# Weight sums of the down product made by copying and accumulating transfers from DRAM to DRAM

## The chip, the cores and the metric

The kernel runs on one core of a Trainium2 chip. The metric is the device time of one execution in microseconds. Before the change the median of three runs is 1769.81 us (1769.12 to 1770.55).

The engines have these names: PE is TensorE's matrix products, PEld its weight loads, DVE is VectorE, ACT is ScalarE, POOL is GpSimd and SP is SyncE. Transfers are issued by SP and by POOL, each in the order of its own queue, and all of them are carried by the same 16 DMA engines.

## What is computed

One step of a one-layer hybrid encoder over 1024 prompt frames and 32 sample frames with 1024 features. The parts that matter here, from the reference:

```
z = rms_norm(x, g_mix) @ w_in          # q, k, v, conv_h, conv_B, conv_C, gate_a, gate_b
a = attn_core(q, k, v) @ w_attn_out    # banded attention, 16 heads, sink softmax
...
x = x + (sigmoid(ga) * a + sigmoid(gb) * bo) @ w_mix_out
... (cross-attention into 256 memory tokens)
x = x + square(relu(rms_norm(x, g_mlp) @ w_up)) @ w_down
```

All inputs are float32, and the products are made from pairs of fp32r parts (a high part "h" and the rest "l"), three matrix products for one.

## The kernel before

The 1056 frames are columns, in three chunks of 384, 384 and 288. The kernel walks through stages, and in each the weights come one 128x1024 tile at a time: SP loads the raw tile, ACT makes its high part (L120), DVE its rest (L121), and TensorE multiplies. The order of the stages is the order of a list of items; within it a planner orders each engine's instructions by a timing model of its own. A call of `pin` puts an instruction behind everything that was traced before it on its engine; instructions traced later may still be planned ahead of it.

The stages that bear on this change, with their places in the trace of before:

- Start and first products, up to about 90 us.
- Attention, about 90 to 360 us. Sixteen host products (projections of q, k, conv and gates) of three chunks each give 48 slots. Into the slots are hung, as events, the parts of 36 attention units: scores (on TensorE, L560 and L561), the softmax (DVE L567, ACT L572, the reciprocal on DVE L576, the scaling of three of four heads on POOL L579 and of one on ACT L581), two slots later the transposes (TensorE L589), one more slot later the values (L601, L602). POOL also writes the sink columns (L563) and some conv and gate products (L631, L662).
- Paired input products, about 360 to 690 us, in which two products of 384 frames share their sub-products (L892 to L894); POOL adds weight tiles for them (L881 to L884).
- Attention output, about 690 to 760 us, then the conv, mix and cross-attention stages, then up and down.

The down product at the end also works with sub-products, in the manner of Strassen's scheme, and needs four combinations of the four blocks of each weight piece. With the blocks s0, s1, s2 and s3 of a piece they are s0+s2+s3, s0+s1+s2+s3, s0+s2 and s2+s3. There are 32 pieces of 128 x 4 x 256 numbers (512 KB), named by (j, t, i). The sums are made ahead, between the work of the first stages, and kept in DRAM in `wsum_d`; the down stage reads them from there by the keys "w_sum" (L138, from 1565 us on).

Before the change POOL makes each piece by one load into SBUF (L742), four additions (L749) and one store to `wsum_d` (L750). The loads go in turn into a tile "ws" of the stage's pool and into "xacc". `sum_step` stores the piece that was loaded last and loads the next one. It is called at 13 slots of the attention stage, by the steps of the paired products, and by the attention output's items, up to about 740 us.

POOL's queue holds its transfers' descriptors in a scratch area whose size is set where the program is made (line 1950, `dynamic_dma_scratch_size=1024`); the change leaves it as it is.

Of the kernel before, what the change touches and what calls it, by code (L numbers as in the profile page):

```python
# [10 lines left out]
F32 = mybir.dt.float32  # L11
F32R = mybir.dt.float32r
AF = mybir.ActivationFunctionType
ALU = mybir.AluOpType
# [4 lines left out]
P = 128  # L19
# [19 lines left out]
def hybrid_step(ctx: ExitStack, tc: tile.TileContext, io):  # L39
    nc = tc.nc  # L40
    act, dve, pool_e, pe, sp = nc.scalar, nc.vector, nc.gpsimd, nc.tensor, nc.sync
# [3 lines left out]
    def nm(s):  # L45
        uid[0] += 1
        return f"{s}_{uid[0]}"

    def opened(name, **kw):
        cm = tc.tile_pool(name=name, **kw)  # L50
        return cm, cm.__enter__()

    def closed(cm):
        cm.__exit__(None, None, None)
# [28 lines left out]
    wsum_d = dram.tile([4, 2, 4, P, 4, 256], F32, name="wsum_d")  # L83
# [4 lines left out]
    def pin(ins):  # L88
        return tc.keep_in_program_order(ins)

    def acc_tile(shape):
        return ps.tile(shape, F32, tag="acc", bufs=n_acc, name=nm("acc"))
# [16 lines left out]
    def item(fn, *keys):  # L109
        plan.append((fn, keys))  # L110
        worder.extend(keys)
# [85 lines left out]
    def xacc_tile():  # L197
        xacc[0] = tp.tile([P, 1056], F32, tag="xacc", name=nm("xacc"))
        return xacc[0]
# [215 lines left out]
    A = {}  # L415

    def open_att():
        closed(st_cm)
        A["cm"], A["pool"] = opened("att", bufs=1, reuse_waits="tile", side="right")
        C["pool"], C["bufs"] = A["pool"], 1  # L420
        W["pool"] = A["pool"]
        for i in range(2):
            for part in "hl":
                at_tile([P, 4 * P], F32R, f"PT{part}{i}")
        at_tile([P, 2, P], F32, "AO", 2)
        at_tile([64, 4, P], F32, "tO")
        at_tile([P, 4, 257], F32, "S", 2)
        at_tile([P, 1060], F32, "u")
        at_tile([P, 4, 256], F32, "ws")
        at_tile([P, 4, 256], F32, "bias")  # L430
        C["cvt"] = A["pool"].tile([P, 4, 4], F32, name="cvt")
        do_KS(0)
        do_KS_rest(0)

    def at_tile(shape, dt, tag, bufs=1):
        pool = kvp if tag in ("kt", "VS", "QA", "QB", "QC") else A["pool"]
        return pool.tile(shape, dt, tag=tag, bufs=bufs, name=nm(tag))
# [70 lines left out]
    def do_KS(kv):  # L508

        hi = at_tile([P, NT], F32R, "KSh", 2)  # L510
        lo = at_tile([P, NT], F32R, "KSl", 2)
        rows = slice(64 * (kv % 2), 64 * (kv % 2) + 64)
        src = ktt[kv // 2]
        for e in range(2):
            act.copy(hi[64 * e : 64 * e + 64], src[rows])
        for e in range(2):
            dve.tensor_sub(lo[64 * e : 64 * e + 64], src[rows], hi[rows].bitcast(F32))
        ksp[kv] = (hi, lo)

    def do_KS_rest(kv):  # L520
        ck = at_tile([P, P], F32, "ck")
        sp.dma_start(ck, io["cache_k"][:, kv])
        b = at_tile([P, 4, 256], F32, "bias")
        sp.dma_start(b, io["bias"][kv])
        bs = at_tile([P, 256], F32, "biass")
        sp.dma_start(bs, io["bias_s"][kv])
        ch = at_tile([P, P], F32R, "ckh")
        cl = at_tile([P, P], F32R, "ckl")
        split(ch, cl, ck)
        ksp[kv] += (ch, cl, b, bs)  # L530
# [156 lines left out]
    def in_emit(tile):  # L687
        which, f = tile
        return gate_emit(which, f) if which in "ab" else conv_emit(which, f)

    def in_col(tile):
        which, f = tile
        return 10 + 8 * "HBCab".index(which) + f

    def do_in(tile, extras=(), chunks=range(3)):
        def fn(w):
            emit = in_emit(tile)
            for c in chunks:
                n = CH[c][1]
                if tile[0] == "B":  # L700
                    conv_taps(tile[1], c)
                a = acc_tile([P, n])
                gemm(a, w, xg[c])
                emit(c, a)
                after(extras, c)

        return fn
# [20 lines left out]
    def at(slot, fn):  # L728
        events.setdefault(slot, []).append(fn)

    W = {}
    pieces = [(j, t, i) for j in range(4) for t in range(2) for i in range(4)]

    def sum_load(acc):
        W["acc"] = acc
        if pieces:
            at = pieces.pop(0)
            if acc:
                t = xacc_tile()[:, :1024].rearrange("p (q c) -> p q c", q=4)
            else:  # L740
                t = W["pool"].tile([P, 4, 256], F32, tag="ws", name=nm("ws"))
            pin(pool_e.dma_start(t, io["w_down"][at]))  # L742
            W["new"] = at, t

    def sum_add(old):
        if old:
            at, t = old
            for to, x, y in ((3, 2, 3), (2, 0, 2), (0, 0, 3), (1, 1, 0)):
                pin(pool_e.tensor_tensor(t[:, to], t[:, x], t[:, y], op=ALU.add))  # L749
            pin(pool_e.dma_start(wsum_d[at], t))  # L750

    def sum_step():
        old = W.pop("new", None)
        sum_load(not W.get("acc", True))
        sum_add(old)

    def sum_done():
        sum_add(W.pop("new", None))

    for kv, starts in enumerate([(0, 1, 2, 4, 5, 6, 8, 9, 10)] * 3 + [(0, 1, 2, 3, 4, 5, 6, 7, 8)]):  # L760
        base = (0, 12, 23, 34)[kv]
        units = [Unit(kv, p) for p in range(9)]
        for unit, k in zip(units, starts):
            at(base + k + 3, unit.values)
        for unit, k in zip(units, starts):
            at(base + k, unit.scores)
        for unit, k in zip(units, starts):
            at(base + k + 2, unit.turn)
        if kv < 3:
            at(base + 7, lambda kv=kv: do_KS(kv + 1))  # L770
            at(base + 11, lambda kv=kv: do_KS_rest(kv + 1))
        for k in ((5, 8, 11), (2, 5, 8, 11), (2, 5, 8, 11), (2, 5))[kv]:
            at(base + k, sum_step)
    at(44, sum_done)
    at(38, lambda: x_raw(0))
    at(40, lambda: x_sums(0))
    at(42, lambda: x_raw(1))
# [206 lines left out]
    def x_steps(i):  # L984
        if i == 0:
            todo = {"B11": lambda: x_issue(1, 4), "W4": lambda: x_issue(1, 3), "W2": lambda: [x_issue(1, 2), x_fetch(2), x_issue(2, 1)]}
        elif i == 1:
            todo = {"W4": lambda: x_issue(2, 4), "W3": lambda: x_issue(2, 3), "W2": lambda: x_issue(2, 2)}
        else:
            todo = {f"W{k}": lambda k=k: x_issue(i + 1, k) for k in (1, 4, 3, 2)}  # L990
            todo["B11"] = lambda: x_fetch(i + 1)

        def after(what):
            if what == "B11":
                sum_done()
            todo.get(what, lambda: None)()
            if what == "W3" and (i % 5):
                sum_load(True)
            if what == "B11" and XP[i][0][0] == "a" and "cv_cm" in S:
                closed(S.pop("r2_cm"))  # L1000
                closed(S.pop("cv_cm"))
                G["pool"] = ctx.enter_context(tc.tile_pool(name="gb", bufs=5, reuse_waits="tile", side="right"))

        return after
# [57 lines left out]
    def open_y(*_):  # L1062
        closed(S["pw_cm"])
        closed(S["tk_cm"])
        W["cm"], W["pool"] = opened("wsum", bufs=1, reuse_waits="tile")
        Y["pool"] = ctx.enter_context(tc.tile_pool(name="ypool", bufs=16, reuse_waits="tile", side="right"))

    todo = []
# [1 line left out]
    def loads(n):  # L1070
        for dst, src, c, k in [todo.pop(0) for _ in range(min(n, len(todo)))]:
            load_split(dst, src, c, k)

    def do_attn_out(f, chunks, steps):
        def fn(w):
            for c in chunks:
                n = CH[c][1]
                a = acc_tile([P, n])
                gemm(a, w, aop[c])
                t = tmp(n)  # L1080
                dve.tensor_mul(t, a, sg[c][f])  # L1081
                sp.dma_start(m1_d[c][:, f], t)
                for at, e in steps:
                    if at == c:
                        e()

        return fn
# [2 lines left out]
    item(lambda: todo.extend((aop, ao_d, c, k) for c in range(3) for k in range(NF)))  # L1090
    last = [t for pair in XP[len(XP) - LATE :] for t in pair]
    for t in last:
        item(do_in(t, [(2, lambda: loads(4)), (2, sum_step)], (2,)), ("w_in", in_col(t)))
    for f in range(4):
        chunks = range(3) if f else (0, 1)
        item(do_attn_out(f, chunks, [(0, sum_step if f == 0 else sum_done)]), ("w_attn_out", f))
    for f in range(4, NF):
        item(do_attn_out(f, (0,), []), ("w_attn_out", f))
    item(lambda: todo.extend((bcp, bc_d, 0, k) for k in range(NF)))
# [3 lines left out]
    for f in range(4, NF):  # L1103
        item(do_attn_out(f, (1,), [(1, lambda: loads(2))]), ("w_attn_out", f))
    run()
    assert not pieces and "new" not in W
    todo.extend((bcp, bc_d, 1, k) for k in range(NF))
    closed(W["cm"])
    closed(x_cm)
    xacc_tile()  # L1110

# [864 lines left out]
```

## Time and profile before

| what | value |
|---|---|
| median of three runs | 1769.81 us |
| the profiled execution | 1767.74 us |
| its span | 1766.0 us |
| PE busy | 1733.7 us, 98% |
| DVE busy | 1213.3 us, 69% |
| POOL busy | 657.9 us, 37% |
| POOL's transfers in all (q0) | 33.56 MB, 5.4% of the 16 DMA engines' span |
| SP's transfers in all (q1) | 276.97 MB, 47.2% |

Busy times are of one profiled execution, which is timed apart from the runs of the median. A group of instructions in the profile stands as line, engine, operation, what it writes and reads, the number of instructions, then their busy time and the mean in ns, then the engine's idle time ahead of them and what ended it. A row of transfers ends with the KB of one and the median time from issue to landing. A row of waits has the total in us, the number of times and the longest. A row of the timeline or the chain begins with the start and the length in us.

### The profile page before, as it was taken

How to read it: one execution, taken by the hardware profiler on the slowest of the kernel's cores; microseconds unless marked ns; L12 is line 12 of the kernel's file. 1: busy time of each engine (PE TensorE's matmuls, PEld its weight loads, DVE VectorE, ACT ScalarE, POOL GpSimd, SP SyncE). 2: the span in 40 equal slices, each digit the busy share in tenths (PEclk: the TensorE clock that was granted, in tenths of full speed). 3: DMA queues.
4: the chain of work that ended last, by engine and by line, in shares of the span. 5: the costliest groups of instructions: out<-in, count | busy, mean ns of one | idle time of the engine just before them, and what ended most of it. 6: DMA issues, size and time to landing. Idle time of an engine off the chain costs nothing.

```text
span 1766.0 us, 30039 instructions
## 1 busy us (share of the span) xinstructions
PE 1733.7 (98%) x11008; PEld 1711.6 (97%) x11008; DVE 1213.3 (69%) x2130; ACT 846.1 (48%) x1625; POOL 657.9 (37%) x702
## 2 busy tenths in 40 slices
PE   8999999999999999999999999999999999999997
PEld 8999999999999999999999999999999999999997
DVE  6768888777887767367576877666666675445665
ACT  8667767852232245144465755642222353432553
POOL 2246675643744534402324241375544300100111
PEclk9999999999999999999999999999999999999998
DMA  5413434442322527789766767744443497544674
GB/s 183 146 58 106 141 114 147 139 153 98 132 86 96 177 102 263 261 255 320 259 218 208 242 219 240 253 166 155 130 139 124 149 316 221 176 152 141 230 240 134
DMA packets 178115, 313.01 MB, mean 177 GB/s; under 512 B 18192, under 2 KB 137776, under 8 KB 177840
## 3 DMA queue, kind: packets, MB, share of 16 engines
q1 hardware_dynamic: 168320, 276.97, 47.2%
q0 software_dynamic: 9216, 33.56, 5.4%
q8 instruction: 86, 1.41, 0.3%
q10 hardware_dynamic: 432, 0.58, 0.1%
q14 instruction: 61, 0.50, 0.1%
HBM read 233.23 MB, written 77.81 MB: 176 GB/s over the span
## 4 chain that ended last, share of the span: by engine, by line
PE 72%; DMA 9%; DVE 6%; ACT 5%; issue 3%; POOL 2%; SPq 1%; POOLq 0%; DVEq 0%; ACTq 0%
PE acc L176 7%; PE acc L178 7%; PE acc L177 7%; PE acc L892 7%; PE acc L894 7%; PE acc L893 7%; PE acc L1707 5%; PE acc L1706 5%; PE acc L1708 5%; PE pa L177 3%; PE pa L178 3%; PE pa L176 3%; DVE wl L121 2%; ACT wh L120 1%; PE pt L589 1%
## 5 line engine op out<-in xcount | busy, mean ns | idle before, releaser
L120 ACT CAST wh<-wr 128x1024 fp32r<-128x1024 f32 (+1 forms) x224 | 234.1, 1045 | 311.4 <-PE acc L1707 77.1
L121 DVE TENSOR_TENSOR wl<-wr,wh 128x1024 fp32r<-128x1024 f32 (+1 forms) x224 | 307.3, 1372 | 93.2 <-ACT wh L120 91.7
L176 PE MATMUL acc<-Y,wh 128*128 128x384 f32 (+1 forms) x624 | 201.9, 324 | 2.6 <-DVE ct L1081 1.5
L178 PE MATMUL acc<-Y,wl 128*128 128x384 f32 (+1 forms) x624 | 201.6, 323 | 0.3 <-DVE wl L121 0.3
L177 PE MATMUL acc<-Y,wh 128*128 128x384 f32 (+1 forms) x624 | 201.6, 324 | 0.0
L253 POOL TENSOR_TENSOR xacc<-xacc,ct 128x384 f32<-128x384 f32 (+1 forms) x62 | 78.0, 1257 | 322.2 <-ACT ct L251 319.8
L176 PE MATMUL acc<-X,wh 128*128 128x384 f32 (+1 forms) x528 | 172.6, 327 | 1.2 <-ACT wh L120 1.2
L177 PE MATMUL acc<-X,wh 128*128 128x384 f32 (+1 forms) x528 | 171.8, 325 | 0.9 <-DVE X L257 0.9
L178 PE MATMUL acc<-X,wl 128*128 128x384 f32 (+1 forms) x528 | 171.0, 324 | 0.0
L176 PEld LDWEIGHTS acc<-Y,wh 128*128 128x128 f32 x624 | 117.0, 188 | 3.9 <-DVE ct L1081 1.9
L178 PEld LDWEIGHTS acc<-Y,wl 128*128 128x128 f32 x624 | 117.2, 188 | 0.6 <-DVE wl L121 0.6
L177 PEld LDWEIGHTS acc<-Y,wh 128*128 128x128 f32 x624 | 117.1, 188 | 0.0
L579 POOL TENSOR_SCALAR S<-S,rec 128x256 f32<-128x256 f32 (+1 forms) x96 | 93.3, 984 | 62.1 <-DVE rec L576 61.9
L1706 PE MATMUL acc<-Y,wh 128*128 128x384 f32 (+1 forms) x352 | 113.1, 321 | 0.2 <-ACT Y L120 0.2
L1707 PE MATMUL acc<-Y,wh 128*128 128x384 f32 (+1 forms) x352 | 113.1, 321 | 0.1
L1708 PE MATMUL acc<-Y,wl 128*128 128x384 f32 (+1 forms) x352 | 112.9, 321 | 0.0
L120 ACT CAST wh<-s 128x1024 fp32r<-128x1024 f32 x54 | 56.6, 1051 | 105.9 <-PE acc L893 72.3
L177 PEld LDWEIGHTS acc<-X,wh 128*128 128x128 f32 x528 | 100.0, 189 | 2.9 <-DVE X L257 1.8
L176 PEld LDWEIGHTS acc<-X,wh 128*128 128x128 f32 x528 | 99.8, 189 | 2.2 <-ACT wh L120 1.4
L178 PEld LDWEIGHTS acc<-X,wl 128*128 128x128 f32 x528 | 99.8, 189 | 1.0 <-DVE wl L121 0.2
L121 DVE TENSOR_TENSOR Y<-ct,Y 128x384 fp32r<-128x384 f32 (+1 forms) x128 | 68.9, 570 | 28.7 <-ACT Y L120 28.5
L120 ACT CAST Y<-ct 128x384 fp32r<-128x384 f32 (+1 forms) x128 | 59.2, 486 | 60.0 <-DMA ct<-bc_d 14.8
(405 smaller groups left out, 5360.3 us busy)
## 6 DMA issues: line engine op xcount, KB each, us to landing
wr<-in_w_in SPq DMA_DIRECT2D x55, 512.0 KB, 3.6
wr<-in_w_up SPq DMA_DIRECT2D x48, 512.0 KB, 3.8
wr<-in_w_down SPq DMA_DIRECT2D x32, 512.0 KB, 4.0
wr<-wsum_d SPq DMA_DIRECT2D x32, 512.0 KB, 3.5
wl<-wl_d SPq DMA_DIRECT2D x28, 512.0 KB, 4.8
wr<-in_w_conv_out SPq DMA_DIRECT2D x24, 512.0 KB, 4.5
wr<-in_w_mix SPq DMA_DIRECT2D x24, 512.0 KB, 4.7
xacc<-in_w_down POOLq DMA_DIRECT2D x21, 512.0 KB, 3.9
```

The source lines that it names most:

```text
L120: act.copy(hi, src)
L121: dve.tensor_sub(lo, src, hi.bitcast(F32))
L176: pe.matmul(out, wh[:, a], hi, start=(k == 0), stop=False)
L177: pe.matmul(out, wh[:, a], lo, start=False, stop=False)
L178: pe.matmul(out, wl[:, a], hi, start=False, stop=(k == len(acts) - 1))
L579: pool_e.tensor_scalar_mul(stl[:, h, :nk], stl[:, h, :nk], rec[:, h : h + 1])
L892: pe.matmul(acc, wh[:, a], hi, start=(start and k == 0), stop=False, skip_group_check=True)
L893: pe.matmul(acc, wh[:, a], lo, start=False, stop=False, skip_group_check=True)
L894: pe.matmul(acc, wl[:, a], hi, start=False, stop=(k == 3), skip_group_check=True)
L1706: pe.matmul(a, wh[:, s], hi, start=(start and k == 0), stop=False, skip_group_check=True)
L1707: pe.matmul(a, wh[:, s], lo, start=False, stop=False, skip_group_check=True)
L1708: pe.matmul(a, wl[:, s], hi, start=False, stop=(stop and k == len(acts) - 1), skip_group_check=True)
```

## The change

The tile "ws", the loads, the additions and the stores are gone. Two pieces are now taken together as 256 rows, which makes 16 pairs, and each pair goes through four phases, all of them transfers of POOL's queue from DRAM to DRAM. Phase 0 copies blocks 0 and 1 of the weights into targets 0 and 1, and blocks 0 and 3 into targets 2 and 3 (512 KB each). Phase 1 adds block 2 to targets 2 and 3, phase 2 adds target 3 to targets 0 and 1, phase 3 adds block 0 to target 1 (256 KB each). The additions are done by the transfers themselves (`accum_op`). The phases of the pairs are interleaved: the list holds phase 3 of one pair, phase 2 of the next, phase 1 of the one after it, phase 0 of a fourth, and so on. The 64 phases are issued in slots 4 to 43 of the attention stage, two in a slot where k % 5 is 0, 2 or 4 and one in the others. The calls in the paired products and in the attention output are taken out.

```diff
@@ open_att
-        W["pool"] = A["pool"]
...
-        at_tile([P, 4, 256], F32, "ws")
@@ the sums
-    def sum_load(acc):
...
-            pin(pool_e.dma_start(t, io["w_down"][at]))
-            W["new"] = at, t
-
-    def sum_add(old):
...
-            for to, x, y in ((3, 2, 3), (2, 0, 2), (0, 0, 3), (1, 1, 0)):
-                pin(pool_e.tensor_tensor(t[:, to], t[:, x], t[:, y], op=ALU.add))
-            pin(pool_e.dma_start(wsum_d[at], t))
...
+    def sum_phase(at, phase):
+        j, t, i = at
+        src, dst = io["w_down"][j, t, i : i + 2], wsum_d[j, t, i : i + 2]
+        src, dst = (x.rearrange("i p q c -> (i p) q c") for x in (src, dst))
+        wide = lambda x: x.to_broadcast([2 * P, 2, 256])
+        if phase == 0:
+            pin(pool_e.dma_start(dst[:, 0:2], src[:, 0:2]))
+            pin(pool_e.dma_start(dst[:, 2:4], src[:, 0:4:3]))
+        elif phase == 1:
+            for q in (2, 3):
+                pin(pool_e.dma_start(dst[:, q], src[:, 2], accum_op=ALU.add))
+        elif phase == 2:
+            for q in (0, 1):
+                pin(pool_e.dma_start(dst[:, q], dst[:, 3], accum_op=ALU.add))
+        else:
+            pin(pool_e.dma_start(dst[:, 1], src[:, 0], accum_op=ALU.add))
+
+    sums = [(j, t, i) for j in range(4) for t in range(2) for i in (0, 2)]
+    phases = [(sums[s - ph], ph) for s in range(len(sums) + 3) for ph in (3, 2, 1, 0) if 0 <= s - ph < len(sums)]
+
+    def sum_step(n=1):
+        for _ in range(min(n, len(phases))):
+            sum_phase(*phases.pop(0))
@@ the attention slots
-        for k in ((5, 8, 11), (2, 5, 8, 11), (2, 5, 8, 11), (2, 5))[kv]:
-            at(base + k, sum_step)
-    at(44, sum_done)
+    for k in range(4, 44):
+        at(k, lambda k=k: sum_step(1 + (k % 5 in (0, 2, 4))))
@@ paired products, attention output
-            if what == "B11":
-                sum_done()
...
-            if what == "W3" and (i % 5):
-                sum_load(True)
...
-        W["cm"], W["pool"] = opened("wsum", bufs=1, reuse_waits="tile")
...
-        item(do_in(t, [(2, lambda: loads(4)), (2, sum_step)], (2,)), ("w_in", in_col(t)))
+        item(do_in(t, [(2, lambda: loads(4))], (2,)), ("w_in", in_col(t)))
...
-        item(do_attn_out(f, chunks, [(0, sum_step if f == 0 else sum_done)]), ("w_attn_out", f))
+        item(do_attn_out(f, chunks, []), ("w_attn_out", f))
...
-    closed(W["cm"])
```

More of the change, by code (lines that the diff above doesn't have):

```diff
@@ L729, in at @@
         events.setdefault(slot, []).append(fn)
-    W = {}
-    pieces = [(j, t, i) for j in range(4) for t in range(2) for i in range(4)]
-    def sum_load(acc):
[L735 to L742, printed above, removed]
-            W["new"] = at, t
-    def sum_add(old):
-        if old:
-            at, t = old
-            for to, x, y in ((3, 2, 3), (2, 0, 2), (0, 0, 3), (1, 1, 0)):
[L749 to L758, printed above, removed]
+    def sum_phase(at, phase):
[19 more added lines that the diff above has]
+            sum_phase(*phases.pop(0))
     for kv, starts in enumerate([(0, 1, 2, 4, 5, 6, 8, 9, 10)] * 3 + [(0, 1, 2, 3, 4, 5, 6, 7, 8)]):
@@ L1105, in hybrid_step @@
     run()
-    assert not pieces and "new" not in W
+    assert not phases
     todo.extend((bcp, bc_d, 1, k) for k in range(NF))
-    closed(W["cm"])
     closed(x_cm)
```

## The prediction

> **What bounds the kernel now.** I read the page's shares of busy time first, then busy time by stretch over the whole span, to see which stretches still have idle TensorE time, because only that can be won.
>
> ```profile
> span 1766.0 us, 30039 instructions
> PE 1733.7 (98%) x11008; PEld 1711.6 (97%) x11008; DVE 1213.3 (69%) x2130; ACT 846.1 (48%) x1625; POOL 657.9 (37%) x702
> ...
> 120.00:350.00 230.00, 229.93 (x1522) 222.84 (x1521) 187.93 (x503) 171.03 (x437) 151.93 (x204) 1.00 0.38 128
> 350.00:440.00 90.00, 87.59 (x543) 86.14 (x543) 64.18 (x92) 40.62 (x68) 37.85 (x39) 1.00 0.38 126
> 440.00:700.00 260.00, 260.00 (x1634) 260.00 (x1634) 199.40 (x264) 89.61 (x126) 127.95 (x141) 1.00 0.40 138
> 700.00:760.00 60.00, 58.31 (x357) 57.67 (x356) 26.31 (x39) 15.79 (x24) 20.43 (x29) 1.00 0.77 256
> ...
> 930.00:1200.00 270.00, 260.22 (x1702) 254.36 (x1701) 197.13 (x347) 151.42 (x293) 107.42 (x95) 1.00 0.66 223
> ```
>
> In the rows by stretch the columns after the length are PE, PEld, DVE, ACT and POOL busy, the granted clock, the DMA share and GB/s. TensorE has no idle time in the attention stretch (120 to 350) or in 440 to 700, 2.4 us in 350 to 440 and 1.7 us in 700 to 760. So the four stretches in which the weight sums are made hold 4.1 us of idle TensorE time in all. The changed code can hardly win more than that; what it can lose has no such limit.
>
> Next I read the groups of POOL in the attention stretch, and the transfers in it.
>
> ```profile
> L579 POOL TENSOR_SCALAR S<-S,rec 128x256 f32<-128x256 f32 x75 | 76.8, 1036 | 39.4 <-DVE rec L576 39.2
> L749 POOL TENSOR_TENSOR ws<-ws 128x256 f32<-128x256 f32 x24 | 19.3, 806 | 0.9
> L749 POOL TENSOR_TENSOR xacc<-xacc 128x256 f32<-128x256 f32 x24 | 19.0, 792 | 1.1
> ...
> L742 POOL DMA_DIRECT2D ws<-in_w_down x7 | 4.2, 593 | 9.4 <-DMA wsum_d<-ws 9.4
> ...
> L750 POOL DMA_DIRECT2D wsum_d<-ws x6 | 3.7, 613 | 1.0 <-POOL ws L749 1.0
> L742 POOL DMA_DIRECT2D xacc<-in_w_down x6 | 3.6, 604 | 0.0
> L750 POOL DMA_DIRECT2D wsum_d<-xacc x6 | 3.6, 600 | 1.5 <-POOL xacc L749 1.5
> ```
>
> POOL's own duty here is the scaling of the softmax rows (L579), and its turn is tight. The next rows show POOL's third scaling, which ends at 340.76, and the transpose on TensorE that reads the result 0.4 us later.
>
> ```profile
> 338.03 2.73 POOL L579 TENSOR_SCALAR S<-S,rec 128x256 f32<-128x256 f32 x3 [0.80 <-DVE rec L576]
> ```
>
> ```profile
> 341.16 0.27 PE L589 MATMUL pt<-ident,S 128*128 128x128 f32 x1
> ```
>
> The chain of waits, read between 308 and 322, passes through POOL without a break, so here POOL is already the engine that the end hangs on.
>
> ```profile
> 309.52 1.81 POOL S L579 x2
> 311.33 0.57 POOL xacc L742
> ...
> 311.93 0.75 POOL ws L749
> ...
> 315.44 1.83 POOL S L579 x2
> ```
>
> **The change, part by part.** *Removed:* 128 additions (L749), 32 loads and 32 stores. Of these the attention stretch has 48 additions (38.3 us) and 25 transfers (15.1 us), 53.4 of POOL's 151.9 us. What stays is 98.5 us in 230, or 105 us in 245. The additions that stood behind 440 are worth nothing, since TensorE is full up to 700; those near 700 to 760 at most the 1.7 us.
>
> *Moved:* every sum now lies in slots 4 to 43 of the attention host items, and none behind them. The first load of before stands at slot 5 and the thirteenth at slot 39:
>
> ```profile
> 123.70 0.77 POOL L742 DMA_DIRECT2D ws<-in_w_down  x1
> ...
> 332.41 0.59 POOL L742 DMA_DIRECT2D ws<-in_w_down  x1
> ```
>
> 208.7 us for 34 slots is 6.1 us a slot, so 40 slots are 245 us. SP issues nothing new, and the reading of the sums starts long after, so no wait moves there. The tile "ws" and a use of "xacc" go; nothing waits for them at these places but POOL.
>
> *Added:* 16 pairs of pieces, each with 2 copies and 2 + 2 + 1 accumulating transfers: 112 transfers instead of the stretch's 25. The issue of one is 0.6 us (593 to 613 ns above, for 128 runs). The new ones have 256 runs, the second copy 512 on its reading side, and no row shows how the issue grows with runs; the ends are 0.6 and, in proportion to 256 runs, 1.2 us. I take 0.6: 67 us. POOL then has 105 + 67 = 172 of 245 us without any hold, which fits, with 73 us to spare.
>
> *Holds.* What decides is whether POOL is held at an issue until an earlier transfer of its own has landed, because the scalings (L579), the sink columns (L563) and the conv and gate products (L662, L631) are queued behind it, and TensorE's transposes wait for the first. Before, this happened 12 times in 64 transfers, 39.7 us, a mean of 3.3 us:
>
> ```profile
> POOL ws L742 <- DMA wsum_d<-ws: 21.5, 6, 6.0
> ...
> POOL xacc L742 <- DMA wsum_d<-xacc: 18.2, 6, 7.2
> ```
>
> There it cost nothing: the 13 loads of this stretch lie 17 us apart (208.7 us over 12), and the 9.4 us of such waits in it left TensorE full. Now there are 2.8 transfers to a slot. Behind another of the same slot stand the second transfer of phases 1 and 2 (32) and the first of a second phase in the 24 slots that run two (24): 56. The two copies of phase 0 I count as flying together. The price of one hold is the landing less the issue. No row shows a transfer from DRAM to DRAM or an accumulating one:
>
> ```profile
> wr<-in_w_in SPq DMA_DIRECT2D x13, 512.0 KB, 3.3
> ws<-in_w_down POOLq DMA_DIRECT2D x7, 512.0 KB, 3.9
> ao_d<-AO SPq DMA_DIRECT2D x27, 128.0 KB, 1.8
> ...
> wsum_d<-ws POOLq DMA_DIRECT2D x6, 512.0 KB, 3.1
> ```
>
> An accumulate of 256 KB reads 512 KB, its source and its target, and writes into DRAM. Its ends are 1.8 us (128 KB, half of what it writes) and 3.9 us (as much read, on this queue); I take 3.5, the mean of POOL's 512 KB load and 512 KB store. A hold is then 2.9 us, and 56 are 162 us. Some of them pass while POOL would have had nothing to do and some while pieces of other work lie between two transfers of one slot; that other work fills 43% of the stretch (105 of 245), and I let a third of the holds vanish in this way: 108 us.
>
> The rows show no hold that comes from anything but a tile's reuse. The Trainium skill ("DMA: Bandwidth & Descriptors", section "Terms") has 16-byte descriptors that GpSimd writes into rings in SBUF; the kernel's 1024 bytes of scratch (line 1950) would be 64 places by it, and by "Collectives: The Full Stack", section "The bandwidth ceiling: the fold count and why AG ≠ RS ≠ AR", an addition reads through two descriptors for each chunk. By both, my estimate for an accumulate is 33 places on each engine, so that two don't fit and the second waits for the first. No run here shows it yet. The first of these pages, section "Anatomy of one DMA — SWDGE (gpsimd) path", also prices a transfer at 2.0 us plus bytes over 436 GB/s, 2.6 us for 256 KB; by that the sum below would end at +2 us. Its price for 512 KB is 3.2 us, where the rows have 3.1 and 3.9.
>
> *Sum.* 105 + 67 + 108 = 280 us of POOL in 245 us: TensorE waits 35 us, spread over the stage. Profiled, 1767.7 + 35 = 1803 us. The profiled execution (span 1766.0 us and 1.7 around it) lies 2.1 us below the runs' median of 1769.8, so the forecast for the median is 1805 us. The far ends: landing 3.9 and nothing hidden is 56 x 3.3 = 185, with 172 it is 357, +112 us, 1882; landing 1.8 is 56 x 1.2 = 67, which fits, +0. If an issue cost 1.2 us, another 67 us would come on top; I leave that outside the range.
>
> **The rivals.**
>
> *No holds, or short ones (no change).* The dependent phases of a pair lie three phases apart, about 11 us, far beyond a landing of 3 to 4 us. If transfers of one phase fly together, or land in 2.6 us (two thirds of 56 x 2.0 = 75 us, about the 73 to spare), POOL keeps up and TensorE stays full: 1769.8. For it speaks that the holds of before left TensorE full, the longest of 6.0 us among them; against it the 0.4 us shown above. The same time comes out if the planner pulls the scalings ahead of the transfers, which are only kept behind what was traced before them: then the transfers run late, into the stage behind, where POOL has room. The change would then not do its work where it says.
>
> *Transfers too slow for the 16 engines (slower).*
>
> ```profile
> q1 hardware_dynamic: 14110, 16.10, 21.4%
> q0 software_dynamic: 3600, 13.11, 16.2%
> ```
>
> Before, 13.11 MB took 16.2% of 230 us, 2.84 us for a MB. 16.8 MB of copies and 21.0 MB of accumulates, counted twice for their two reads, are 58.7 MB, 167 us, 68% of 245 us; with the other queue's 21% that is just below full, and no loss. If an accumulate costs twice that again, it is 286 us and 52 of the other queue, 338 in 245: +93, about 1863. Nothing in the rows asks for the factor.
>
> *Faster.* The additions are gone, POOL is never late, and all 4.1 us of idle time in 350 to 440 and 700 to 760 goes: 1765.7. If the new plan also takes half of the 9.8 us in 930 to 1200, 1760.8. For it speaks that POOL's additions lie on the chain at 311 to 316; against it that TensorE was full there, and that the longest waits of TensorE in those two stretches are on DVE:
>
> ```profile
> PE acc L176 <- DVE ct L1081: 1.5, 1, 1.5
> ...
> PE acc L892 <- DVE ct L678: 1.0, 1, 1.0
> ```
>
> **How the numbers follow.** Holds that overfill POOL 0.47; transfer engines full 0.10; no holds, short holds or transfers put late 0.32; faster 0.11. A measurement of this kernel tells about 0.2%, 3.5 us, from no change. Slower by more than that: 0.57 from the first two, a little more for small losses in the third and a little less for a first case that ends near 0, so 0.57. Within: 0.32. Faster: 0.11. Range: the likeliest case alone is 1774 to 1882; down to the no-change case and part of the faster one it is 1764, and I keep 1882 above, leaving out some 5% below and 13% above.
>
> **What would show it.** Right: POOL's DMA rows longer than 0.6 us, or idle time before them that ends at a transfer to wsum_d; TensorE in 120 to 400 with tens of us idle before the transposes (L589), released by POOL; later stretches as before, only shifted. The additions (L749) gone from 440 to 760 with TensorE unchanged there shows that they cost nothing. Wrong: POOL issues of 0.6 us with no idle time before them and TensorE still full, or the accumulates lying behind 400. If TensorE waits for weights instead (L138 landing late, DMA share above 0.9), the second rival holds.

## The result and the profile after

The changed kernel takes 2029.78 us (median; 2026.03 to 2031.54) beside 1770.18 us for the kernel before in the same session: a ratio of 1.1476, with an interval of 1.1462 to 1.149. It is 259.6 us slower. The forecast was slower, by the right mechanism, but only by 35 us; the time lies far outside the stated range.

First the page's shares of busy time and the busy time by stretch, after the change:

```profile
span 2024.1 us, 29970 instructions
PE 1794.0 (89%) x11008; PEld 1754.8 (87%) x11008; DVE 1197.7 (59%) x2130; ACT 848.6 (42%) x1629; POOL 600.4 (30%) x622
...
115.00:640.00 525.00, 331.84 (x1780) 304.63 (x1778) 200.09 (x544) 192.08 (x477) 195.48 (x255) 0.78 0.54 108
640.00:700.00 60.00, 51.01 (x302) 50.70 (x303) 44.78 (x60) 23.19 (x35) 21.75 (x17) 0.90 0.32 111
700.00:1020.00 320.00, 320.00 (x2004) 320.00 (x2003) 219.55 (x312) 109.25 (x157) 63.22 (x63) 1.00 0.33 107
```

The columns of a row by stretch are those of the prediction's rows. From 700 us on TensorE is full through the paired products, as before (320.0 of 320 us). The loss lies in the attention stage, which now fills 115 to 640. The scalings of the softmax rows on POOL (one line of code, L579 before and L577 after, and its first and last start) date it:

```profile
L579 POOL TENSOR_SCALAR S<-S,rec x96: 593/924/1994, 95.3 to 349.2; 128x256 f32<-128x256 f32 x84, 128x128 f32<-128x128 f32 x12
```

```profile
L577 POOL TENSOR_SCALAR S<-S,rec x96: 592/948/2308, 94.3 to 608.3; 128x256 f32<-128x256 f32 x84, 128x128 f32<-128x128 f32 x12
```

The last scaling starts 259.1 us later, as much as the whole loss. What POOL did in between stands in its groups between 115 and 640; the part behind the bar is its idle time ahead of the group, and what ended it:

```profile
L577 POOL TENSOR_SCALAR S<-S,rec 128x256 f32<-128x256 f32 x76 | 76.9, 1174 | 13.3 <-DVE rec L574 13.2
L740 POOL DMA_DIRECT2D wsum_d<-in_w_down x32 | 29.8, 930 | 96.4 <-issue 90.9 <-DMA wsum_d<-in_w_down 5.5
L743 POOL DMA_DIRECT2D wsum_d<-wsum_d x32 | 29.3, 917 | 108.0 <-issue 108.0
L745 POOL DMA_DIRECT2D wsum_d<-in_w_down x16 | 15.3, 954 | 58.8 <-issue 46.1 <-DMA wsum_d<-wsum_d 9.9 <-PE acc L178 1.5
L737 POOL DMA_DIRECT2D wsum_d<-in_w_down x16 | 15.0, 935 | 49.0 <-issue 43.7 <-PE acc L178 4.5 <-PE pt L587 0.7
L736 POOL DMA_DIRECT2D wsum_d<-in_w_down x16 | 14.4, 899 | 0.0
```

POOL stands idle for 312 us ahead of its own transfers, 289 of them put down to "issue" (77 times), that is, to nothing that the profile names. With the 195 us of its busy time that is 484 of the 525 us; only 17 us of idle time stand ahead of the scalings and 23 us ahead of transfers for other reasons. The low share of 30% busy time hides this, because waiting at an issue isn't counted as busy. The stage's other engines wait for it: ACT's exponentials (L570) for the sink columns (L561), which stand in POOL's order behind the transfers, and TensorE's transposes for the scalings of POOL and of ACT. The two rows of TensorE are 142 of its 193 idle us in this stretch:

```profile
ACT S L570 <- POOL S L561: 185.8, 23, 15.0
PE pt L587 <- POOL S L577: 95.3, 24, 12.8
PE pt L587 <- ACT S L579: 46.4, 7, 12.7
```

The transfers that hold it, with KB each and the median time to landing, and POOL's timeline over the first of them:

```profile
wsum_d<-in_w_down POOLq DMA_DIRECT2D x32, 512.0 KB, 5.7
...
wsum_d<-in_w_down POOLq DMA_DIRECT2D x48, 256.0 KB, 5.1
```

```profile
123.17 1.03 POOL L740 DMA_DIRECT2D wsum_d<-in_w_down  x1 [5.47 <-DMA wsum_d<-in_w_down]
128.16 0.90 POOL L740 DMA_DIRECT2D wsum_d<-in_w_down  x1 [3.96 <-issue]
...
129.03 3.26 POOL L577 TENSOR_SCALAR S<-S,rec 128x256 f32<-128x256 f32 x3
132.02 0.85 POOL L736 DMA_DIRECT2D wsum_d<-in_w_down  x1
133.60 0.93 POOL L737 DMA_DIRECT2D wsum_d<-in_w_down  x1 [0.73 <-PE pt L587]
...
140.25 1.00 POOL L743 DMA_DIRECT2D wsum_d<-wsum_d  x1 [5.51 <-issue]
144.68 0.90 POOL L743 DMA_DIRECT2D wsum_d<-wsum_d  x1 [3.43 <-issue]
```

Here the second accumulating transfer of a phase starts 5.0 us after the first, which landed 4.7 us after its issue; further down it is 4.4 us. The scalings at 129.03 stand behind it in POOL's order. A plain copy (L736, 132.02) is issued 3.9 us after an accumulating transfer that takes 5.1 us to land, and isn't held.

### The profile page after: what moved, and what is told of

Read it like the earlier page. It is cut to its first block, busy times and chain, and to the rows that moved or that the text cites. A ratio compares the mean times of both kernels' runs of the same rounds, so it can differ in the third digit from the quotient of the medians.

```text
span 2024.1 us, 29970 instructions
## 1 busy us (share of the span) xinstructions
PE 1794.0 (89%) x11008; PEld 1754.8 (87%) x11008; DVE 1197.7 (59%) x2130; ACT 848.6 (42%) x1629; POOL 600.4 (30%) x622
## 3 DMA queue, kind: packets, MB, share of 16 engines
q0 software_dynamic: 26368, 37.76, 11.1%
## 4 chain that ended last, share of the span: by engine, by line
PE 63%; issue 16%; POOL 9%; DVE 4%; DMA 4%; ACT 3%; SPq 0%; POOLq 0%; ACTq 0%; DVEq 0%
PE acc L176 6%; PE acc L177 6%; PE acc L178 6%; PE acc L885 6%; PE acc L887 6%; PE acc L886 6%; PE acc L1694 5%; PE acc L1693 5%; PE acc L1695 5%; POOL S L577 4%; PE pa L177 2%; PE pa L176 2%; PE pa L178 2%; POOL wsum_d L740 1%; DVE wl L121 1%
## 5 line engine op out<-in xcount | busy, mean ns | idle before, releaser
L587 PE MATMUL pt<-ident,S 128*128 128x128 f32 x248 | 61.0, 349 | 158.1 <-POOL S L577 95.3
L587 PEld LDWEIGHTS pt<-ident,S 128*128 128x128 f32 x248 | 38.2, 173 | 175.0 <-POOL S L577 105.1
L176 PE MATMUL acc<-X,wh 128*128 128x384 f32 (+1 forms) x528 | 183.0, 347 | 0.8 <-ACT wh L120 0.8
L177 PE MATMUL acc<-X,wh 128*128 128x384 f32 (+1 forms) x528 | 181.3, 343 | 1.1 <-DVE X L257 1.1
L178 PE MATMUL acc<-X,wl 128*128 128x384 f32 (+1 forms) x528 | 181.0, 343 | 0.0
L570 ACT ACTIVATE S<-S,nmx 128x257 f32<-128x257 f32 (+1 forms) x132 | 63.9, 487 | 194.0 <-POOL S L561 185.8
L177 PEld LDWEIGHTS acc<-X,wh 128*128 128x128 f32 x528 | 108.6, 206 | 3.1 <-DVE X L257 1.9
L176 PEld LDWEIGHTS acc<-X,wh 128*128 128x128 f32 x528 | 109.0, 206 | 2.4 <-ACT wh L120 1.0
L178 PEld LDWEIGHTS acc<-X,wl 128*128 128x128 f32 x528 | 108.0, 205 | 0.9 <-DVE wl L121 0.2
L577 POOL TENSOR_SCALAR S<-S,rec 128x256 f32<-128x256 f32 (+1 forms) x96 | 91.5, 1092 | 38.6 <-DVE rec L574 38.5
```

Source lines behind the costliest of these rows:

```text
L176: pe.matmul(out, wh[:, a], hi, start=(k == 0), stop=False)
L177: pe.matmul(out, wh[:, a], lo, start=False, stop=False)
L178: pe.matmul(out, wl[:, a], hi, start=False, stop=(k == len(acts) - 1))
L577: pool_e.tensor_scalar_mul(stl[:, h, :nk], stl[:, h, :nk], rec[:, h : h + 1])
```

## The experiments

The pattern suggests a theory with a count in it, which carries the prediction's estimate on. It assumes that POOL writes a transfer's descriptors (the entries that tell the DMA engines what to move) into the 1024 bytes, as 64 places of 16 bytes for each of the 16 engines. A transfer of 256 runs (contiguous pieces) would put 16 runs on each engine and one closing entry, so a plain copy would take 17 places; an accumulating transfer, which reads twice, 33; and the copy with a strided source (512 runs) also 33. No trace shows these places; the runs below test what follows from the count. Two of 33 are 66 and wouldn't fit, 33 and 17 are 50 and would. **Theory A** is that POOL is held whenever the next transfer doesn't fit, until enough earlier ones have landed. **Theory B** is that accumulating transfers go one at a time by nature. **Theory C** is that the 16 engines or DRAM are too slow for accumulating.

### More room

```diff
-    nc = _bacc.Bacc("TRN2", target_bir_lowering=False, num_devices=1, dynamic_dma_scratch_size=1024)
+    nc = _bacc.Bacc("TRN2", target_bir_lowering=False, num_devices=1, dynamic_dma_scratch_size=1728)
```

> The changed kernel with POOL's descriptor scratch of 1728 bytes instead of 1024 (all that the stage with the least free memory leaves), nothing else. Theory A (room): POOL is held at an issue because the descriptors of an accumulating transfer fill more than half of the room, so the next one waits until the one before has landed. With 1728 bytes three fit, and the holds of 289 us fall below 100 us: POOL's other work of 105 us, 112 issues of 0.92 us and 60 us of holds give about 270 us in the attention stretch of 245, some 1795 us (1768 to 1840). Theory B (one at a time by nature: POOL's queue never has two accumulating transfers under way) and theory C (the 16 DMA engines or DRAM are too slow for the accumulating): no change, 2020 to 2035 us.

It took 1829.66 us beside 1770.31: 200 us of the 260 are gone. The idle time ahead of the transfers that nothing in the profile names, with the number of times, and the stretch:

```profile
  issue: 51.2, 37
```

```profile
115.00:360.00 245.00, 228.44 (x1433) 217.93 (x1432) 161.14 (x442) 143.38 (x361) 152.39 (x195) 0.97 0.89 184
```

The holds fall from 289 to 51 us, and B falls: the same accumulating transfers in the same order go several at a time. The second number from the right in the stretch is the share of the 16 DMA engines: they are now 89% busy, and a 256 KB accumulate lands 6.6 us after its issue instead of 5.1. This run doesn't show what keeps the other 60 us.

The count of A was then tested with the smallest step that should matter, 64 bytes more, 68 places instead of 64.

```diff
-    nc = _bacc.Bacc("TRN2", target_bir_lowering=False, num_devices=1, dynamic_dma_scratch_size=1024)
+    nc = _bacc.Bacc("TRN2", target_bir_lowering=False, num_devices=1, dynamic_dma_scratch_size=1088)
```

> The changed kernel with the scratch of 1088 bytes instead of 1024: 64 bytes, four places of 16 bytes more. Theory A with the count of 33 places for an accumulating transfer on each of the 16 engines: two need 66, which don't fit into 64 places and do fit into 68. So the second transfer of phases 1 and 2 (32 of the 77 holds) isn't held any more, while every third still is; the holds fall from 289 to 130 to 200 us and the time to 1880 to 1960 us. If the room acts gradually, or by something else than this count, four places more change next to nothing: 2010 to 2035 us.

```profile
  issue: 129.6, 56
```

1889.0 us, with holds at the lower edge of what was expected: 64 bytes took 141 us off the kernel, more than half of the loss. A room that acted gradually would not do that. The order of POOL's instructions shows the step itself: two accumulating transfers can now go out one right behind the other, as in this row, 1.97 us for both, and the plain copy behind them, which was never held with 1024 bytes, is now held 11 times:

```profile
123.01 1.97 POOL L740 DMA_DIRECT2D wsum_d<-in_w_down  x2 [5.20 <-DMA wsum_d<-in_w_down]
```

```profile
POOL wsum_d L736 <- issue: 32.4, 11, 4.4
```

Both follow from the count: two of 33 fit into 68 places and not into 64, and they leave no room for the 17 of a copy, while a single one left 31. That a hold appears where none was before sets the count apart from a room that merely got larger. With 1728 bytes the holds ahead of this copy are down to 3.8 us in 4.

### Transfers of half the size

Every transfer is cut in two, one of 128 rows for each piece:

```diff
+        two = [(io["w_down"][j, t, i + n], wsum_d[j, t, i + n]) for n in range(2)]
...
         elif phase == 1:
             for q in (2, 3):
-                pin(pool_e.dma_start(dst[:, q], src[:, 2], accum_op=ALU.add))
+                for src, dst in two:
+                    pin(pool_e.dma_start(dst[:, q], src[:, 2], accum_op=ALU.add))
```

> The changed kernel with every transfer cut into two of 128 rows each, one per piece: 224 transfers, same bytes, same phases, scratch of 1024 bytes. Theory A: an accumulating transfer takes half the room, so three fit; POOL's 105 us of other work, 224 issues of 0.8 us and perhaps 60 us of holds are 345 us in 245: about 1870 us (1800 to 1930), less than the changed kernel. Theory B: 160 accumulating transfers one after another, each at least 3.3 us from issue to landing, are over 530 us, no better than the changed kernel: 2030 to 2200 us. Theory C: same bytes, about 2030 us.

1905.98 us, with 89.0 us of holds in 76: twice the transfers and 124 us less time than the changed kernel. By the expectations B would have made it no faster, and C would have left it the same. The largest item in POOL's time is now the issuing itself, 224 instructions of about 0.87 us, 194 us.

### Plain copies of the same shape

```diff
-                pin(pool_e.dma_start(dst[:, q], src[:, 2], accum_op=ALU.add))
+                pin(pool_e.dma_start(dst[:, q], src[:, 2]))
```

(and so for the other accumulating lines; the sums are then not formed)

> The changed kernel with the 80 accumulating transfers made plain copies of the same shape, so the sums are not formed; number, size, order and pins of the transfers are the same. If accumulating is what costs (A: two reads per run take twice the room; B; C), the holds fall below 100 us and the time to 1770 to 1810 us. If the cost is in the number of transfers from DRAM to DRAM and their issue alone, it stays above 1950 us.

1817.88 us, a little above the range, with 75.8 us of holds in 30. The same run with the larger room:

> Plain copies in place of the accumulating transfers (the sums are not formed), in the changed kernel's order and slots, with the scratch of 1728 bytes. With 1024 bytes this took 1817.9 us with 76 us of holds. Theory A: the copies take 17 places each (33 for the strided one) of 107, so the holds fall below 15 us and the time to 1768 to 1785 us. If what is left there came from landing times or from the number of issues, it stays above 1800 us.

```profile
  issue: 1.9, 1
```

```profile
L577 POOL TENSOR_SCALAR S<-S,rec x96: 592/917/1906, 94.9 to 395.1; 128x256 f32<-128x256 f32 x84, 128x128 f32<-128x128 f32 x12
```

```profile
115.00:360.00 245.00, 242.75 (x1590) 235.33 (x1589) 174.82 (x478) 165.15 (x415) 151.02 (x221) 1.00 0.73 202
360.00:440.00 80.00, 57.94 (x290) 50.60 (x289) 48.69 (x93) 40.99 (x86) 36.71 (x45) 0.77 0.48 142
```

The holds vanish as A says (1.9 us), but the time doesn't: 1799.89 us, 15 us above what was expected. So something beside the room costs some 32 us (1767.71 us for the kernel before in the same session). POOL still waits 30 us in 13 places for the phase before to land (a wait that the program needs), and issues 112 transfers. The last scaling starts at 395.1 instead of 349.2. TensorE is nearly full up to 360 with the host products, but in 360 to 440 it has 22 us idle. My reading is that the attention units fall behind the host products, TensorE takes the products first, and the units that are left at the end have nothing beside them; no run separates this from the load on the DMA engines (73%).

### Without the accumulating transfers

Only the copies of phase 0 are left, and three of the four sums are not formed:

```diff
-        elif phase == 1:
-            for q in (2, 3):
-                pin(pool_e.dma_start(dst[:, q], src[:, 2], accum_op=ALU.add))
...
```

> The changed kernel with the 32 copies of phase 0 alone and no accumulating transfer, so three of the four sums are not formed. It bounds what taking POOL's additions away can be worth: by the idle time of TensorE in the stretches of the old sums at most 4 us below the kernel before, 1766 to 1771 us. If the planner's new order costs anything by itself, it shows here as a time above 1773 us.

> The copies of phase 0 alone (three of the four sums are not formed), repeated against the kernel before. One run gave 1765.8 us against 1770.3. If POOL's additions in the stages behind cost TensorE's idle time, it is faster by 0.15 to 0.3%; if that was chance, within 0.1%.

1765.8 us at first, and 1765.86 us against 1767.71 in the repetition: a ratio of 0.9987, with an interval of 0.9977 to 0.9996. Taking all of POOL's additions away, and paying for no sum but the copies, is worth 0.04 to 0.23%, at most some 4 us. The planner's new order cost nothing in these two runs, which are without the 80 accumulating transfers.

### One transfer at a time

The pieces' phases are cut into units (two copies, or one accumulating transfer). 40 units go into the attention slots, one each, the rest into the paired products.

```diff
-        at(k, lambda k=k: sum_step(1 + (k % 5 in (0, 2, 4))))
+        at(k, sum_step)
...
             todo.get(what, lambda: None)()
+            if what in ("B11", "W1", "W4", "W3"):
+                sum_step()
```

> The same 112 transfers with the scratch of 1024 bytes, but one unit at a time (the two copies of a pair, or one accumulating transfer): 40 units in slots 4 to 43 of the attention stage, the other 56 in the paired products behind it, at four places of each pair. Theory A (room): accumulating transfers that stand a landing time (5.1 us) apart don't hold POOL; slots are 6.1 us apart, so the holds fall from 289 us to below 60 us, none of them long, and the time to 1768 to 1785 us. Theory C (accumulating itself is too slow, or it slows the weights' loads): TensorE waits in the paired products too, over 1800 us.

```profile
  issue: 182.5, 58
```

```profile
115.00:360.00 245.00, 240.62 (x1561) 232.78 (x1560) 177.99 (x499) 171.74 (x432) 132.44 (x173) 0.99 0.56 127
360.00:440.00 80.00, 72.08 (x445) 69.06 (x443) 51.62 (x86) 40.81 (x77) 35.10 (x36) 1.00 0.57 145
440.00:700.00 260.00, 236.53 (x1423) 234.93 (x1423) 170.83 (x236) 70.80 (x94) 108.12 (x122) 0.95 0.63 138
```

1816.89 us, a ratio of 1.0271 (1.025 to 1.0293). The expectation was wrong: 182.5 us of holds, not below 60. In the attention stage the spacing did most of what it should (TensorE 240.6 of 245 us), though 49 us of holds are left up to 440. The other 133 us fall into 440 to 720, in the paired products, where the units came too close, and there POOL's weight sums are queued behind a held transfer: ACT's cast of a weight tile waited for one of them 52.0 us in 7.

```profile
ACT wh L120 <- POOL s L873: 52.0, 7, 17.2
```

So a place where POOL has spare time isn't a safe place, if something with a due time stands behind the hold.

With the spacing and the room together:

> The one-unit spacing of the run above with the scratch of 1728 bytes. Theory A: now three accumulating transfers fit, so nothing holds POOL; 1764 to 1772 us, at best the 1765.8 us that the copies of phase 0 alone took. If it is no better than with 1024 bytes, what the spacing leaves is not a matter of room.

1772.36 us, just above the expected 1764 to 1772, a ratio of 1.002 (1.0008 to 1.0031), with 13.1 us of holds. The room makes 44.5 us of difference at this spacing. Of the 0.2% that are left the plainest trace is in 360 to 440, where TensorE had 5.9 us idle instead of 1.8 before the change. A last run took the units away from there:

```diff
-    for k in range(4, 44):
+    for k in range(4, 40):
...
-            if what in ("B11", "W1", "W4", "W3"):
+            if i and what in ("B11", "W1", "W4", "W3", "W2"):
```

> The one-unit spacing with 1728 bytes, with no unit in slots 40 to 43 and none beside the first pair of the paired products, where the earlier spacing left TensorE idle 5.9 us of 80 (360 to 440 us); the units that leave there go to a fifth place of the later pairs. If POOL's late scalings at the end of the attention stage are what was left, 1764 to 1769 us, level with the kernel before or up to 0.2% faster; if it was the load on the 16 DMA engines, unchanged at about 1772 us.

1772.17 us, a ratio of 1.0017 (1.0008 to 1.0026): no change, though with the scalings of the stage's end free of transfers. TensorE still had 4.7 us idle in that stretch, and the share of the DMA engines there fell from 0.72 to 0.56. The holds in the whole kernel were 30.5 us in 16. POOL's late scalings aren't the cause; whether the load on the DMA engines is, wasn't shown. No version made its sums by transfers and beat the kernel before.

## Why the prediction was wrong in size

**What bounded the kernel, and what could be won:** right. At most 4.1 us were said to be there; without any accumulating transfer the gain is 2 us (0.04 to 0.23%).

**The mechanism:** right. POOL is held at its issues by earlier transfers of its own, the scalings and sink columns stand behind, and TensorE's transposes wait. The rivals fell: POOL was held, the transfers lay where the change puts them, and nothing was won. Transfers too slow for the engines was priced at +93 us; the engines were 54% busy in the slow stretch, so it didn't set this time; with more room their share is 89%.

**The sum:** three terms of it were too small. It had 105 + 67 + 108 = 280 us of POOL; the trace has 92 us of other work, 104 us of issues and 289 us of holds, 485, and 40 us of other idle time, in 525.

- *The holds* are the step that failed most, 108 against 289 us. The number was 56, one for each transfer behind another of its slot; there are 77, since POOL was also held at the first of a slot behind transfers of the slots before, and at 12 of the 16 strided copies, which were counted as flying together with the copy ahead of them. One was priced at 2.9 us, from a landing of 3.5; a mean hold is 289 / 77 = 3.75 us, since an accumulate of 256 KB lands in 5.1 us and a copy of 512 KB in 5.7. Even the upper end that was taken for a landing, the 3.9 us of a load of 512 KB, was below.
- *A third of the holds was let vanish* behind other work of POOL, by the mean share of that work in the stretch (43%). But the timeline of POOL has nothing between two transfers where the 56 were counted: all 56 come directly behind another transfer, and 47 of them were held, 205.8 us, 4.4 each, about the landing of 5.1 less the issue of 0.93 in full. (Eight of the other nine are plain copies of phase 0, which by the count fit.) The rest are the 12 strided copies, 43.7 us, and 18 of the 40 transfers that stand behind scalings or other work, 39.2 us, 2.2 each; there the other work did shorten the holds. Without the discount and with the measured number, size and work the same sum is 92 + 104 + 289 = 485 us, 240 us over the 245 of the stretch, close to the loss. The "far end" of +112 us left the discount out but kept the small number and the small price.
- *The issue* takes 0.93 us, not 0.6: 37 us more. In the run with plain copies and 1024 bytes those of the same 256 runs took 0.57 us (median) and the strided copy of 512 runs 0.91, so the 256 runs aren't what costs; the longer issue came with accumulating and with the strided source. The half-size accumulates, with half the runs, still took at least 0.80 us. The plain copy of phase 0 (L736) also took 0.90 us in the changed kernel, but 0.60 with plain copies behind and ahead of it; why isn't shown.

**The estimate that spoke against the change** was the one to follow. The 33 places, worked out from the Trainium skill ("DMA: Bandwidth & Descriptors", section "Terms", and "Collectives: The Full Stack", section "The bandwidth ceiling: the fold count and why AG ≠ RS ≠ AR"), agree with the step from 64 to 68 places, 141 us. The price of the first page's section "Anatomy of one DMA — SWDGE (gpsimd) path", 2.6 us for 256 KB, doesn't hold here: 5.1 us for the accumulating transfers.

## What to carry to other kernels

Before moving work onto an engine's transfer queue, count the descriptors that each transfer needs on one engine against the room that the kernel reserves: a transfer that takes more than half of the room (here, by the estimate, 33 of 64 places) lets only one of its kind be under way at a time, and the engine that issues it stands still with everything queued behind it. In a profile such an engine looks idle; read its idle time ahead of its own transfers before calling it free. When a discount for overlap decides between no loss and a large one, give the sum without the discount as the upper end, and discount only those waits that have other work of the engine directly ahead of them: here none of the 56.

## What the runs showed of the hardware

Most of the idle time of POOL ahead of its transfers that the profile puts down to "issue" is a wait for room: it fell from 289 us to 130 and 51 as the room went from 1024 to 1088 and 1728 bytes, with the same instructions in the same slots.

An accumulating transfer is dearer than its bytes. The two queue rows are those of the changed kernel and of the one with phase 0 alone:

```profile
q0 software_dynamic: 26368, 37.76, 11.1%
```

```profile
q0 software_dynamic: 4608, 16.78, 3.4%
```

Of all 16 engines' time that is 224.7 us (11.1% of 2024.1) less 60.0 us (3.4% of 1763.7) for 80 accumulating transfers, 2.1 us each, in 272 packets each (26368 less 4608, over 80). The same 80 as plain copies took 0.9 us each (7.4% of 1816.1 less the same 60.0), in 80 packets.

TensorE's granted clock was 0.78 in the slow stretch, where it waited, and 1.00 again from 700 us on. Its busy time in the whole span grew from 1733.7 to 1794.0 us for the same 11008 products. This didn't set the time as far as the trace shows, since POOL's work and holds fill 484 of the 525 us, but whoever reads the busy time of a waiting TensorE should look at the clock first.
